# A decoder trunk on one core: the front starts from the normalised input, and the residual is transposed in the output projection

## The chip, the core and the metric

The kernel runs on one core of one Trainium2 chip. The metric is device time of one execution in microseconds (us). An engine in the text is one of the core's five instruction streams, each of which works its list in order: PE (TensorE: products and transposes), DVE (VectorE), ACT (ScalarE), POOL (GpSimd) and SP (SyncE, which only issues DMAs; ACT and POOL can issue some too).

## What is computed

Two layers over 1024 tokens of width 1024, with 16 learned "meta" tokens put ahead of them (1040 in all). This change touches the first half of layer 0, a Mamba-2 mixer with its RMS norm:

```python
h = concat([meta, x])                         # 1040 x 1024
u = rmsnorm(h, ssd_norm)                      # h * rsqrt(mean(h*h) + eps) * gain
z, xbc, dt_raw = split(u @ w_in, ...)         # 2048, 3072 and 32 columns
xbc = silu(causal_dwconv(xbc))
dt = softplus(dt_raw + dt_bias)               # the time steps, one per token and head
...                                           # state space scan, gate, group norm
h = h + hg @ w_out                            # 2048 -> 1024: the output projection
```

The rest (the gated FFNs, the attention of layer 1, the last norm) is the same in both kernels.

## The kernel before

**Layout.** Activations lie feature-major: 128 features on the partitions, tokens along the free axis. The tokens are cut into three *tiles* of 348, 348 and 344 (`TT`), and each tile into three *chunks* of 116 (`CH`, nine chunks c0 to c8). Every float32 product is made of three passes of a faster format: an operand is split into a high part and a low remainder (`uh`, `ul`; `wh`, `wl` for weights), and `mm3` (L193 to L195) multiplies high by high, high by low and low by high. ACT writes the high parts, DVE (for activations) or POOL (for weights, L98, in quarters) the remainders.

**The front (`load_x`).** The nine chunks of x arrive token-major, in two DMAs each (112 rows and 4, `by_rows`, L405), the odd ones from SP's queue and the even ones from ACT's own. For each tile, `stream(j)` squares the three chunks with a sum along the row (L364 on DVE, L366 on ACT), transposes the *raw* chunks on PE (L371, eight groups k of 128 features, three transposes each), copies them out of PSUM as `h` (L374 and L376) and multiplies `h` by the 32 columns `wdt` of the time steps as a plain float32 product (L377, into `dtr`). With the third tile, the finished rows `h` go to DRAM as `h0_d` (L379), eight rows of 520 KB. `token_rstd` turns the sums into one factor per token (L244 to L250). Then `scaled(j)` multiplies the chunks by their factors (L388), transposes them again (L393, into `xr`) and writes `uh` (L303, ACT) and `ul` (L304, DVE), the operands of the input projection. The time steps, made from raw rows, are multiplied by the factors later, in `dt_path` (L460).

**After the front.** `stream` (the method at L603) runs the input projection block by block: a block is 128 output columns, three tiles of 24 products (`pj`, L193 to L195), then a convolution (one ACT instruction L320, three DVE instructions L323) and a silu (L512). Group 0 has six blocks. Between them `dt_path` makes the decays: `acs` (L480), `end` (L481), a transposition `rows` (L493), a round over DRAM, and the tile `D`. The state space part begins with the first `cb` (L665) on PE, after 18 tiles of group 0 and one more tile of products; from there on a hand-written order mixes the scan with further projections.

**The output projection (`out_proj`).** Three passes g over eight row blocks f, each with three tiles of 12 products (`acc`). In the first pass `h[f]` is fetched from `h0_d` (L419), and every pass adds its products to `h[f]` on DVE (L431). A last stage on two halves of the tokens follows.

Outside the hand-written part, a scheduler places the instructions of each engine by its own estimate of when operands are there; what it made of the program is what the rows of order show. PSUM banks come from small pools: `mm` (2 banks), `sm` (3), `lg` (2), `ex` (1). The big SBUF rows are 28 slots of one pool (`Q`), the weights three slots of each kind.

Of the kernel before, what the change touches and what calls it, by code (L numbers as in the profile page):

```python
# [13 lines left out]
P = 128  # L14
D = 1024
# [54 lines left out]
ORD = ((0, 0), (1, 0), (0, 1), (1, 1), (0, 2), (1, 2))  # L70
# [3 lines left out]
PIECE = 256  # L74

# [25 lines left out]
class Trunk:  # L101
    def __init__(self, ctx, tc, a):
# [10 lines left out]
        self.open = []  # L113
        self.consts()
# [56 lines left out]
    def load_w(self, src, n, gain=None, out=None):  # L171
# [8 lines left out]
        nc.scalar.activation(wh[:, :n], w32[:, :n], AF.Copy)  # L180
# [9 lines left out]
    def mm3(self, out, wh, wl, uh, ul, first, last, joins=False, tie=None):  # L190

        mm = self.nc.tensor.matmul
        self.behind(mm(out, wh, uh, start=first, stop=False, skip_group_check=joins), tie, "behind the sums of squares")  # L193
        mm(out, wh, ul, start=False, stop=False, skip_group_check=joins)  # L194
        mm(out, wl, uh, start=False, stop=last, skip_group_check=joins)  # L195
# [41 lines left out]
    def token_rstd(self, ss, m, k, eps=EPS, y=None, src=None):  # L237
# [6 lines left out]
        nc.vector.tensor_scalar(ss[:m, :k], (ss if src is None else src)[:m, :k], 1.0 / D, eps, op0=ALU.mult, op1=ALU.add)  # L244
        nc.scalar.activation(y[:m, :k], ss[:m, :k], AF.Ln)
        nc.scalar.activation(y[:m, :k], y[:m, :k], AF.Exp, scale=-0.5)
# [48 lines left out]
    def parts(self, t, u, s0, n, g, eng=None):  # L295
# [6 lines left out]
        else:  # L302
            nc.scalar.activation(h, t, AF.Copy, scale=g)  # L303
            nc.vector.scalar_tensor_tensor(l, t, g, h.bitcast(F32), op0=ALU.mult, op1=ALU.subtract)  # L304
# [22 lines left out]
    def load_x(self, pool, mx):  # L327
# [5 lines left out]
        wdt = self.wp.tile([P, 1024], F32, tag="w32", name="wdt")  # L333
        self.ln_exp()
        d = self.dp.tile([KD, P, L], F32, tag="h0_d", name="h0_d")
        r9 = mx.tile([P, 3, 3], F32, tag="r9", name="r9")
        dt = self.ex("dtr")
        xs = []
        for c, (t0, n) in enumerate(CH):
# [4 lines left out]
            else:  # L344
                self.by_rows(nc.sync if c % 2 else nc.scalar, xt[:n, :], a["x"][t0 - META : t0 - META + n, :], n)
            if c == 0:
                nc.sync.dma_start(wdt[:, : KD * H], a["w_dt"])
                v = wdt[:, : KD * H].rearrange("p (k h) -> p k h", k=KD)
                nc.gpsimd.tensor_tensor(v, v, self.par("ssd_norm", 0, KD).unsqueeze(2).to_broadcast([P, KD, H]), op=ALU.mult)
# [4 lines left out]
        hs = [self.Q("h") for _ in range(KD)]  # L354

        def stream(j):
            s0, nn = TT[j]
            x3 = xs[3 * j : 3 * j + 3]
            for i in range(3):
                c = 3 * j + i  # L360
                n = CH[c][1]
                t = self.wp.tile([P, D], F32, tag="wl", name=self.nm("junk"))
                if c in SQD:
                    nc.vector.scalar_tensor_tensor(t[:n, :], x3[i][:n, :], 1.0, x3[i][:n, :], op0=ALU.mult, op1=ALU.mult, accum_out=ss[:n, c : c + 1])  # L364
                else:
                    nc.scalar.activation(t[:n, :], x3[i][:n, :], AF.Square, accum_out=ss[:n, c : c + 1])  # L366
            for k in range(KD):
                ps = self.lg("xT")
                for i in range(3):
                    n = CH[3 * j + i][1]  # L370
                    nc.tensor.transpose(ps[:, i * CB : i * CB + n], x3[i][:n, k * P : k * P + P], self.ident[:n, :n])  # L371
                h = hs[k][:, s0 : s0 + nn]
                if k % 2:
                    nc.scalar.activation(h, ps[:, :nn], AF.Copy)  # L374
                else:
                    nc.vector.tensor_copy(h, ps[:, :nn])  # L376
                nc.tensor.matmul(dt[j * H : j * H + H, :nn], wdt[:, k * H : k * H + H], h, start=k == 0, stop=k == KD - 1)  # L377
                if j == 2:
                    nc.sync.dma_start(d[k], hs[k][:, :L])  # L379
            self.token_rstd(ss[:, 3 * j : 3 * j + 3], CB, 3, y=r9[:, :, j])  # L380

        def scaled(j):
            s0, nn = TT[j]
            x3 = xs[3 * j : 3 * j + 3]
            for i, t in enumerate(x3):
                n = CH[3 * j + i][1]
                r = r9[:n, i : i + 1, j]
                nc.vector.tensor_scalar(t[:n, :], t[:n, :], r, None, op0=ALU.mult)  # L388
            for k in range(KD):
                ps = self.sm("xr")  # L390
                for i in range(3):
                    n = CH[3 * j + i][1]
                    nc.tensor.transpose(ps[:, i * CB : i * CB + n], x3[i][:n, k * P : k * P + P], self.ident[:n, :n])  # L393
                self.parts(ps[:, :nn], u[k], s0, nn, self.par("ssd_norm", k))

        for step, j in ORD:
            (scaled if step else stream)(j)
        return d, u, dt, r9
# [25 lines left out]
    def accumulate(self, h, f, s0, n, w, ks, front=0, bank=None, base=0):  # L424
# [6 lines left out]
        self.nc.vector.tensor_tensor(h[f][:, o], h[f][:, o], ps[:, :n], op=ALU.add)  # L431


    def dt_path(self, ps, r9, cp):
# [168 lines left out]
    def stream(self, blocks, w0=None):  # L603
# [11 lines left out]
        for n in range(3 * len(todo)):  # L615
# [5 lines left out]
            if n in calls:  # L621
                calls.pop(n)()
# [1208 lines left out]
```

## Time and profile before

| what | value |
|---|---|
| three runs, us | 2891.38, 2893.07, 2890.8 (median 2891.38) |
| the profiled execution, us | 2892.33 |
| its span (first to last instruction), us | 2890.5 |
| PE busy | 2834.6 us, 98% of the span |
| DVE busy | 2096.3 us, 73% |
| ACT and POOL busy | 1628.0 us and 1610.4 us, 56% each |
| mean granted PE clock | 0.997 |
| DMA | 278.70 MB, 90 GB/s of HBM traffic over the span |

The span is 1.8 us shorter than the execution's own time: what lies around the first and the last instruction. The profile lists busy time by engine, the span in 40 slices, the chain of work that ended last, the groups of instructions by source line, and who waited for whom. A row of the timeline gives the start, the duration, the engine, the line, the operation, output<-input, and how often it stands there in sequence; in brackets the idle time before it and what ended that. The end of a product is modelled and reaches into the next one, so that the step from start to start is what a product costs in a row.

### The profile page before, as it was taken

How to read it: one execution, taken by the hardware profiler on the slowest of the kernel's cores; microseconds unless marked ns; L12 is line 12 of the kernel's file. 1: busy time of each engine (PE TensorE's matmuls, PEld its weight loads, DVE VectorE, ACT ScalarE, POOL GpSimd, SP SyncE). 2: the span in 40 equal slices, each digit the busy share in tenths (PEclk: the TensorE clock that was granted, in tenths of full speed). 3: DMA queues.
4: the chain of work that ended last, by engine and by line, in shares of the span. 5: the costliest groups of instructions: out<-in, count | busy, mean ns of one | idle time of the engine just before them, and what ended most of it. 6: DMA issues, size and time to landing. Idle time of an engine off the chain costs nothing. (4 is left out here: it accounts for less than half of the span.)

```text
span 2890.5 us, 58592 instructions
## 1 busy us (share of the span) xinstructions
PE 2834.6 (98%) x21835; PEld 2701.9 (93%) x21835; DVE 2096.3 (73%) x4044; ACT 1628.0 (56%) x3392; POOL 1610.4 (56%) x2430
## 2 busy tenths in 40 slices
PE   7999999999999999999999999999999999999998
PEld 4999999999999999999999999999798999999888
DVE  5676666668387667666886888888749776767776
ACT  4455544544265656565335888888736565555433
POOL 2265555552429888858743222222363888885882
PEclk9999999999999999999999999999999999999999
DMA  5233333343213222244132222222332222225331
GB/s 168 75 107 95 117 94 117 114 156 135 81 60 97 81 81 76 81 161 164 52 114 78 57 68 66 62 63 54 134 117 74 81 76 79 81 81 183 110 102 66
DMA packets 128265, 278.70 MB, mean 96 GB/s; under 512 B 14787, under 2 KB 58828, under 8 KB 127980
## 3 DMA queue, kind: packets, MB, share of 16 engines
q1 hardware_dynamic: 122028, 261.70, 28.7%
q10 hardware_dynamic: 4112, 6.56, 0.7%
q0 software_dynamic: 1840, 6.70, 0.6%
q8 instruction: 172, 2.82, 0.4%
q14 instruction: 113, 0.93, 0.1%
HBM read 204.63 MB, written 55.36 MB: 90 GB/s over the span
## 5 line engine op out<-in xcount | busy, mean ns | idle before, releaser
L98 POOL TENSOR_TENSOR wl<-w,wh 128x256 fp32r<-128x256 f32 x768 | 682.0, 918 | 377.3 <-ACT wh L180 299.8
L193 PE MATMUL pj<-uh,wh 128*128 128x348 f32 (+2 forms) x1536 | 500.0, 326 | 2.7 <-DVE qs L1469 1.9
L194 PE MATMUL pj<-ul,wh 128*128 128x348 f32 (+2 forms) x1536 | 494.7, 322 | 0.0
L195 PE MATMUL pj<-uh,wl 128*128 128x348 f32 (+2 forms) x1536 | 491.5, 320 | 0.0
L193 PE MATMUL p<-bh,fh 128*128 128x262 f32 (+1 forms) x1408 | 400.4, 285 | 5.5 <-DVE p L1118 5.5
L195 PE MATMUL p<-bh,fl 128*128 128x262 f32 (+1 forms) x1408 | 400.1, 284 | 1.9 <-POOL fl L98 1.9
L194 PE MATMUL p<-bl,fh 128*128 128x262 f32 (+1 forms) x1408 | 398.7, 283 | 0.0
L98 POOL TENSOR_TENSOR fl<-x,fh 128x256 fp32r<-128x256 f32 x352 | 265.6, 786 | 191.9 <-ACT fh L1055 161.5
L193 PE MATMUL p<-bh,wh 128*128 128x262 f32 (+1 forms) x1040 | 295.7, 284 | 1.5 <-ACT ft L1115 1.5
L194 PE MATMUL p<-bl,wh 128*128 128x262 f32 (+1 forms) x1040 | 295.8, 284 | 1.2 <-DVE bl L979 1.2
L195 PE MATMUL p<-bh,wl 128*128 128x262 f32 (+1 forms) x1040 | 295.0, 284 | 0.0
L193 PEld LDWEIGHTS pj<-uh,wh 128*128 128x128 f32 x1536 | 288.3, 188 | 5.0 <-issue 1.9
L194 PEld LDWEIGHTS pj<-ul,wh 128*128 128x128 f32 x1536 | 288.9, 188 | 1.1
L195 PEld LDWEIGHTS pj<-uh,wl 128*128 128x128 f32 x1536 | 288.6, 188 | 0.6 <-issue 0.6
L323 DVE SCALAR_TENSOR_TENSOR c<-p,params,c 128x260 f32<-128x260 f32 (+1 forms) x528 | 248.5, 480 | 53.3 <-ACT c L320 46.7
L193 PEld LDWEIGHTS p<-bh,fh 128*128 128x128 f32 x1408 | 267.1, 190 | 6.3 <-DVE p L1118 5.9
L195 PEld LDWEIGHTS p<-bh,fl 128*128 128x128 f32 x1408 | 267.0, 190 | 2.8 <-POOL fl L98 2.5
L194 PEld LDWEIGHTS p<-bl,fh 128*128 128x128 f32 x1408 | 267.5, 190 | 0.1
L1115 ACT ACTIVATE ft<-p 128x262 f32<-128x262 f32 (+1 forms) x352 | 132.5, 382 | 175.0 <-DVE p L1118 111.2
L195 PE MATMUL acc<-gh,wl 128*128 128x260 f32 (+1 forms) x672 | 213.5, 320 | 2.8 <-POOL wl L98 2.6
L193 PE MATMUL acc<-gh,wh 128*128 128x260 f32 (+1 forms) x672 | 210.9, 320 | 3.1 <-DVE h L1279 3.1
L194 PE MATMUL acc<-gl,wh 128*128 128x260 f32 (+1 forms) x672 | 213.9, 319 | 0.0
(332 smaller groups left out, 7898.9 us busy)
## 6 DMA issues: line engine op xcount, KB each, us to landing
w<-in_w_up SPq DMA_DIRECT2D x88, 512.0 KB
w<-in_w_down SPq DMA_DIRECT2D x44, 512.0 KB
w<-in_w_in SPq DMA_DIRECT2D x40, 512.0 KB
E<-ea_d SPq DMA_DIRECT2D x32, 464.0 KB
D<-acs_d SPq DMA_DIRECT2D x32, 420.5 KB
g<-c SPq DMA_DIRECT2D x88, 130.0 KB
g<-c SPq DMA_DIRECT2D x88, 128.0 KB
b<-g SPq DMA_DIRECT2D x16, 520.0 KB
```

What stands on the lines that cost most here:

```text
L98: eng.tensor_tensor(out[:, c], x[:, c], y[:, c], op=op)
L193: self.behind(mm(out, wh, uh, start=first, stop=False, skip_group_check=joins), tie, "behind the sums of squares")
L194: mm(out, wh, ul, start=False, stop=False, skip_group_check=joins)
L195: mm(out, wl, uh, start=False, stop=last, skip_group_check=joins)
L323: ins = nc.vector.scalar_tensor_tensor(out, ps[:, o + i : o + i + n], wcol(i), out, op0=ALU.mult, op1=ALU.add)
L1115: nc.scalar.activation(s[:, :N], ps[:, :N], AF.Copy)
```

## The change

1. **The raw pass goes.** L371, L374, L376, L377 and the eight stores L379 are no longer there, nor the multiplication by the factors in `dt_path`. Instead the 32 columns of the time steps are split into high and low parts (`wd`, laid into zeroed tiles with 96 columns per product, so that each token tile lands in its own 32 rows of `dtr`), and multiplied by `uh` and `ul` with `mm3`: 24 products per tile, 72 in all.
2. **Order of loads.** The first three chunks, then the first weight block and `w_dt`, then the other six chunks. ACT issues only c0 and c2; SP issues everything else.
3. **Tile by tile.** A generator (`steps`) makes tile j: factors for two chunks, then for the third; chunks scaled in place, shared by DVE and ACT; eight transposition groups; `uh` and `ul`. The squares of the next tile are placed between them. Between tiles stand one tile of products of the first block, and the time-step products. Ordering ties (`behind`) hold the scheduler to this.
4. **The residual.** `h[f]` in the first pass is copied from PSUM (`new`). In the second and third pass the input x is read a second time, in feature blocks of 128 columns (`load_rows`, eight DMAs in pieces of 512 bytes), eight 128x128 transposes per block put it into two PSUM banks (`add_rows`), and DVE adds it to `h[f]`. The meta tokens go over a small DRAM tile, `meta_d`.

What it does to the order. PE's list begins as follows before (`x_108`, `x_114`, `x_117` are the chunks of tile 0; `xT` the raw transposes, `xr` the scaled ones), first its start, and then the place where the first block begins:

```order
L371 MATMUL xT_183<-ident,x_108 128x116
L371 MATMUL xT_189<-ident,x_108 128x116
L371 MATMUL xT_183<-ident,x_114 128x116
L371 MATMUL xT_189<-ident,x_114 128x116
L371 MATMUL xT_183<-ident,x_117 128x116
L371 MATMUL xT_189<-ident,x_117 128x116
L377 MATMUL dtr_107<-h_169,wdt 32x348
```

```order
L193 MATMUL pj_549<-uh_137,wh_532 128x352
L377 MATMUL dtr_107<-h_171,wdt 32x348
L371 MATMUL xT_320<-ident,x_120 128x116
L371 MATMUL xT_320<-ident,x_123 128x116
L371 MATMUL xT_320<-ident,x_126 128x116
L393 MATMUL xr_260<-ident,x_108 128x116
L393 MATMUL xr_260<-ident,x_114 128x116
L393 MATMUL xr_260<-ident,x_117 128x116
L194 MATMUL pj_549<-ul_138,wh_532 128x352
```

In the changed kernel (`x_106`, `x_110`, `x_113` are tile 0, `xr` its scaled transposes) PE's list has, after eight small transposes of the meta tokens:

```order
L402 MATMUL xr_221<-ident,x_113 128x116
L402 MATMUL xr_227<-ident,x_113 128x116
L402 MATMUL xr_233<-ident,x_113 128x116
L195 MATMUL pj_280<-uh_139,wh_118 128x352
L402 MATMUL xr_239<-ident,x_106 128x116
L402 MATMUL xr_239<-ident,x_110 128x116
L402 MATMUL xr_239<-ident,x_113 128x116
L196 MATMUL pj_280<-ul_140,wh_118 128x352
L197 MATMUL pj_280<-uh_139,wl_119 128x352
L195 MATMUL pj_280<-uh_141,wh_118 128x352
```

The raw transposes and the float32 products are gone from between the block's products; the first block's first tile follows the first tile's scaled transposes directly, and the 24 products into `dtr` stand behind it.

ACT's list before: five DMAs more than in the changed kernel stand ahead of its first square.

```order
L405 DMA x_117<-in_x 4x1024
L405 DMA x_123<-in_x 112x1024
L405 DMA x_123<-in_x 4x1024
L405 DMA x_129<-in_x 112x1024
L405 DMA x_129<-in_x 4x1024
L405 DMA x_135<-in_x 112x1024
L366 ACTIVATE junk_177,ss_101<-x_108 116x1024
```

And in the changed kernel, with the path of the third chunk (`x_113`) behind the copy of the first weights:

```order
L491 DMA x_113<-in_x 4x1024
L377 ACTIVATE junk_190,ss_101<-x_106 116x1024
L433 ACTIVATE mT_186<-mT_177 128x128
L247 ACTIVATE r_104<-ss_101 116x2
L248 ACTIVATE r_104<-r_104 116x2
L377 ACTIVATE junk_194,ss_101<-x_113 116x1024
L247 ACTIVATE r_104<-ss_101 116x1
L248 ACTIVATE r_104<-r_104 116x1
L417 ACTIVATE wh_118<-w_0_116 128x1024
L394 ACTIVATE x_113<-x_113,r_104 116x512
```

ACT's first square is no longer behind the issue of later chunks; those DMAs stand in SP's list.

SP's list of the changed kernel, in the third pass of the output projection: the six blocks of x that this pass adds (`xb`) stand together, ahead of the pass's last three weight loads.

```order
L466 DMA xb_7834<-in_x 128x8x128
L466 DMA xb_7837<-in_x 128x8x128
L466 DMA xb_7902<-in_x 128x8x128
L466 DMA xb_7905<-in_x 128x8x128
L176 DMA w_1006_8113<-in_w_out_f 128x512
L176 DMA w_1012_8162<-in_w_out_f 128x512
L176 DMA w_1018_8211<-in_w_out_f 128x512
```

The core of the diff:

```diff
+LOADS = {(1, 0): (0, 1), (2, 0): (2, 3), (2, 1): (4, 5), (2, 2): (6, 7)}
+ADDS = {(1, 2): (0,), (1, 3): (1,), (2, 1): (2,), (2, 2): (3, 4), (2, 3): (5, 6), (2, 4): (7,)}
...
+        for c in range(3):
+            load(c)
+        w32 = self.wp.tile([P, 1024], F32, tag="w32", name="w32_0")
+        nc.sync.dma_start(w32, first)
...
+        nc.sync.dma_start(wdt, a["w_dt"])
+        for c in range(3, 9):
+            load(c)
...
+        def tile(j):
+            a, b, c = range(3 * j, 3 * j + 3)
+            if j == 0:
+                for x in (a, b, c):
+                    square(x, None)
+            factors(j, 0, 2)
+            scale(a, [(nc.vector, 0, D)])
+            factors(j, 2, 1)
+            scale(b, [(nc.scalar if j else nc.vector, 0, D)], None if j else self.first_factor)
+            if j == 0:
+                self.behind(nc.scalar.activation(w0[0], w32, AF.Copy), self.last_exp, "behind the factors")
+                pieces(nc.gpsimd, w0[1], w32, w0[0].bitcast(F32), ALU.subtract)
+            scale(c, [(nc.vector, 0, D // 2), (nc.scalar, D // 2, D)])
+            transposed(j, range(KD // 2))
+            if j < 2:
+                hi, lo = made[j, KD // 2 - 1]
+                square(a + 3, hi)
+                square(b + 3, lo)
+            transposed(j, range(KD // 2, KD))
+            if j < 2:
+                square(c + 3, made[j, KD - 1][0])
...
+            for j in range(3):
+                s0, n = TT[j]
+                c = slice(HALO + s0, HALO + s0 + n)
+                for k in range(KD):
+                    w = slice(2 * H + G * k - H * j, 2 * H + G * k - H * j + G)
+                    self.mm3(dt[:G, :n], wd[0][:, w], wd[1][:, w], u[k][0][:, c], u[k][1][:, c], j == k == 0, j == 2 and k == KD - 1, tie=self.last_mm)
+                if j < 2:
+                    tile(j + 1)
...
+    def load_rows(self, f):
+        t = self.Q("xb")
+        self.nc.sync.dma_start(t[:, :SEQ].rearrange("p (c q) -> p c q", q=P), self.a["x"][:, f * P : f * P + P].rearrange("(c p) q -> p c q", p=P))
+        self.nc.gpsimd.dma_start(t[:, SEQ : SEQ + META], self.meta_d[f])
+        return t
+
+    def add_rows(self, h, t):
+        nc = self.nc
+        banks = [self.sm("xT") for _ in range(2)]
+        tie = self.last_mm
+        for c in range(SEQ // P):
+            ins = nc.tensor.transpose(banks[c // 4][:, c % 4 * P : c % 4 * P + P], t[:, c * P : c * P + P], self.ident)
+            self.behind(ins, tie, "behind the block's products")
+            tie = None
+        m = h[:, HB : HB + META]
+        nc.vector.tensor_tensor(m, m, t[:, SEQ : SEQ + META], op=ALU.add)
+        for i, ps in enumerate(banks):
+            x = h[:, HB + META + 512 * i : HB + META + 512 * i + 512]
+            nc.vector.tensor_tensor(x, x, ps, op=ALU.add)
...
-        self.nc.vector.tensor_tensor(h[f][:, o], h[f][:, o], ps[:, :n], op=ALU.add)
+        if new:
+            self.nc.vector.tensor_copy(h[f][:, o], ps[:, :n])
+        else:
+            self.nc.vector.tensor_tensor(h[f][:, o], h[f][:, o], ps[:, :n], op=ALU.add)
...
             u, dt, heads, w0, front = self.load_x(pool, mx, self.a["w_in"][DI // P])
             dt = self.dt_path(dt, heads, mx)
             next(front)
             rows = [[] for _ in range(4)]
             group = self.stream(self.in_group(u, 0, rows[0]), w0, True)
             for _ in range(3):
                 next(group)
                 next(front)
             next(dt)
...
                 if g == 0:
-                    h[f] = self.fetch(hd[f], "h", front=HB)
+                    h[f] = self.Q("h")
+                    self.nc.gpsimd.tensor_copy(h[f][:, :HB], self.zero[:, :HB])
+                for k in LOADS.get((g, f), ()):
+                    rows[k] = self.load_rows(k)
...
+                for k in ADDS.get((g, f), ()):
+                    self.add_rows(h[k], rows.pop(k))
```

More of the change, by code (lines that the diff above doesn't have):

```diff
@@ L382, in scaled @@
[L382 to L394, printed above, removed]
@@ L396, in load_x, with square @@
-        for step, j in ORD:
-            (scaled if step else stream)(j)
-        return d, u, dt, r9
+        G = 3 * H
+        wd = [self.Q("wd", F32R) for _ in range(2)]
+        for t in wd:
+            nc.gpsimd.memset(t.bitcast(F32), 0.0)
+        taps = [t[:, 2 * H : 2 * H + KD * G].rearrange("p (k h) -> p k h", h=G)[:, :, :H] for t in wd]
+        made = {}
+        def square(c, tie):
+            n = CH[c][1]
+            t = self.wp.tile([P, D], F32, tag="wl", name=self.nm("junk"))
+            x, acc = xs[c][:n, :], ss[:n, c : c + 1]
+            if c in SQD:
+                ins = nc.vector.scalar_tensor_tensor(t[:n, :], x, 1.0, x, op0=ALU.mult, op1=ALU.mult, accum_out=acc)
+            else:
+                ins = nc.scalar.activation(t[:n, :], x, AF.Square, accum_out=acc)
+            self.behind(ins, tie, "behind the tile in front")
@@ new lines, in transposed @@
+        def transposed(j, ks):
+            s0, nn = TT[j]
+            for k in ks:
+                ps = self.sm("xr")
+                for i, x in enumerate(xs[3 * j : 3 * j + 3]):
+                    n = CH[3 * j + i][1]
+                    t = nc.tensor.transpose(ps[:, i * CB : i * CB + n], x[:n, k * P : k * P + P], self.ident[:n, :n])
+                    if j:
+                        self.behind(t, self.last_mm, "behind the products in front")
+                made[j, k] = self.parts(ps[:, :nn], u[k], s0, nn, self.par("ssd_norm", k))
@@ L797, in mixer @@
                     pass
[L798 removed]
+        return rows[3][:4], yd, list(zip(y0[1], y0[0]))
     def fetch_y(self, d):
```

136 lines of the change are left out of this document (74 added, 62 removed).

## The prediction

> **What bounds the kernel now.** I read the page first, then who waited for whom on PE, then the timeline at the start.
>
> ```profile
> PE 2834.6 (98%) x21835; PEld 2701.9 (93%) x21835; DVE 2096.3 (73%) x4044; ACT 1628.0 (56%) x3392; POOL 1610.4 (56%) x2430
> ...
> PE   7999999999999999999999999999999999999998
> ```
>
> PE is busy nearly always; the first slice (72 us) alone shows less. So two things count here: when PE gets useful work at the start, and how much PE work there is. PE's longest waits, over the whole run:
>
> ```profile
> PE xT L371 <- DMA x<-in_x: 10.7, 2, 5.8
> ...
> PE dtr L377 <- ACT h L374: 3.0, 1, 3.0
> ...
> PE acc L193 <- DVE h L431: 0.6, 2, 0.4
> ```
>
> The first two stand in the front, the third in the first pass of the output projection. PE's timeline of the front, and where the scan begins:
>
> ```profile
> 14.09 0.84 PE L371 MATMUL xT<-ident,x 116*128 116x116 f32 x3
> 17.94 1.37 PE L377 MATMUL dtr<-h,wdt 128*32 128x348 f32 x2 [3.01 <-ACT h L374]
> ...
> 24.91 0.52 PE L371 MATMUL xT<-ident,x 116*128 116x116 f32 x3
> ...
> 28.72 0.46 PE L393 MATMUL xr<-ident,x 116*128 116x116 f32 x3
> ...
> 32.78 0.40 PE L193 MATMUL pj<-uh,wh 128*128 128x352 f32 x1
> ...
> 35.19 0.77 PE L377 MATMUL dtr<-h,wdt 128*32 128x348 f32 x2
> 35.90 0.52 PE L371 MATMUL xT<-ident,x 116*128 116x116 f32 x3
> ...
> 36.25 0.46 PE L393 MATMUL xr<-ident,x 116*128 116x116 f32 x3
> ...
> 131.01 0.33 PE L195 MATMUL pj<-uh,wl 128*128 128x352 f32 x1
> 131.18 0.27 PE L665 MATMUL cb<-ident,xbc 128*116 128x128 f32 x1
> ...
> 131.49 0.60 PE L669 MATMUL px<-ident,xbc 128*116 128x128 f32 x4
> 131.84 0.41 PE L193 MATMUL pj<-uh,wh 128*128 128x352 f32 x1
> ```
>
> The scaled transposes begin at 28.7 and the first `cb` stands at 131.2; PE is dense between, 102.5 us. Two prices are read here: a product costs 0.16 from start to start, and four 128x128 transposes 0.35, with the product behind them 0.41 long, about 0.1 more. Three transposes took 0.84 at 14.1 and 0.52 at 24.9: PE runs slow until about 24.2, though the granted clock of that stretch is recorded as 1.00 (the column ahead of the DMA share in the next fence).
>
> **The end of the front, before and after.** `cb` comes after 18 tiles of group 0 and one more in both programs, and the code from there on is the same. So the front's gain is how much earlier PE reaches it.
>
> *Removed from the dense stretch:* the raw groups.
>
> ```profile
> 0.00:28.70 28.70, 6.89 (x30) 1.00 0.75 200
> 28.70:62.00 33.30, 7.36 (x44) 1.00 0.46 177
> ```
>
> ```profile
> 28.70:62.00 33.30, 11.75 (x32) 1.00 0.46 177
> ```
>
> These are L371 (two stretches) and L377. The busy times, 7.4 + 11.8 = 19.1 us, overlap with neighbours and are the upper bound. From start to start a raw group costs 0.71 (35.19 to 35.90) and 0.35 (to 36.25), 1.06 in all, of which 0.1 is the switch to other work, which partly stays; 16 of the 24 `dtr` products (two recorded instructions each) stand in this stretch: 17.0 us, and 15.4 without the switch, the lower bound. I take 17.0, since steps are what PE spends. 85.5 remain.
>
> *Added:* 72 products for the time steps at 0.16 = 11.5 us, all on PE in this stretch, with no cover.
>
> *The new start.* Landing is read from the queue, where a load waits for a slot of an earlier one:
>
> ```profile
> 0.84 14.41 ACTq L405 DMA_DIRECT2D x<-in_x  x9
> ...
> 10.68 0.31 SPq L405 DMA_DIRECT2D x<-in_x  x1
> 11.01 0.32 ACTq L405 DMA_DIRECT2D x<-in_x  x1
> ...
> 15.36 1.06 ACT L366 ACTIVATE junk<-x 116x1024 f32<-116x1024 f32 x1 [13.27 <-DMA x<-in_x]
> ```
>
> The second and third chunks landed just before 10.68 and 11.01. ACT's first square ran at 15.4 only because its own DMA issues stood ahead of it; in the new order four issues do. The weight block now travels beside these chunks in place of two later ones, much the same bytes, so I take 10.4 and 10.9. Then the chain runs on these prices:
>
> ```profile
> 12.64 1.22 DVE L364 SCALAR_TENSOR_TENSOR junk<-x 116x1024 f32<-116x1024 f32 x1
> ...
> 19.05 0.21 ACT L246 ACTIVATE r<-r 116x3 f32<-116x3 f32 x1
> ...
> 19.68 0.17 DVE L249 TENSOR_SCALAR tb<-tb 116x3 f32<-116x3 f32 x1
> 19.88 0.16 DVE L250 TENSOR_TENSOR r<-r,tb 116x3 f32<-116x3 f32 x1
> ...
> 26.97 1.05 ACT L180 ACTIVATE wh<-w 128x1024 fp32r<-128x1024 f32 x1
> ```
>
> ```profile
> L388 DVE TENSOR_SCALAR x<-x,r x9: 742/752/1292, 26.6 to 58.1; 116x1024 f32<-116x1024 f32 x8, 112x1024 f32<-112x1024 f32 x1
> ```
>
> Square of c1 with its read-out 1.3 (11.7), sum, logarithm and exponential 0.2 each (12.3), four small DVE steps at 0.2 (13.1), two chunks scaled at 0.75 with the next sum between (14.8). Meanwhile ACT squares c2 (to 13.6), makes its factor (14.4) and copies the weights (15.4); four DVE steps (15.6), two half scales (16.2), transposes, first `uh`: **first product at 17.2**, against 32.8 before.
>
> From 17.2, at slow PE prices (0.84 a group of transposes, 0.32 a product), tile 0 still needs five groups and 24 products, 4.2 + 7.7 = 11.9. Before, PE sped up 6.2 us after its dense run began (17.94 to about 24.2). The same here: 6.2 slow, then 5.7 at half price, 2.9: tile 0's projection ends at 26.2. The suppliers are no slower than that once PE is fast:
>
> ```profile
> L304 DVE SCALAR_TENSOR_TENSOR ul<-xr,params,uh 128x348 fp32r<-128x348 f32 (+1 forms) x24 | 13.3, 570 | 8.8 <-ACT uh L303 8.8
> ```
>
> That is 0.57 a group, about 0.49 from start to start in a row. [...]
>
> *Sum.* Done by 26.2 are 24 products (3.8) and eight groups of scaled transposes. A group costs at least 0.25 + 0.08 for the switch, and at most
>
> ```profile
> 28.70:73.00 44.30, 11.46 (x72) 8.44 (x72) 1.00 0.38 145
> ```
>
> 11.46 / 24 = 0.48; I take 0.37, 3.0 us. So 85.5 + 11.5 - 6.8 = 90.2 remain, plus 0.7, since ACT makes the second block's weights between two of tile 1's `uh`: `cb` at 26.2 + 90.9 = 117.1, **14.1 us earlier**. Cover between tiles: tile 0's time-step products (24 x 0.16 = 3.8 us) hide the scaling of tile 1's last chunk, which by the same prices ends within 0.3 of them; nothing is left over, and what DVE or ACT lose there, PE loses. Tile 2 has the second block's products as cover. I allow 0 to 4 us here. The decays' round over DRAM has cover too:
>
> ```profile
> 103.59 0.70 SPq L637 DMA_DIRECT2D D<-acs_d  x2
> ...
> 133.78 1.60 DVE L648 TENSOR_SCALAR D<-D,cols 116x116 f32<-116x116 f32 x8
> ```
>
> `D` was asked for 27.6 us before `cb`; in the new order PE's `rows` stands 123 rows ahead of `cb` rather than 195, which at 0.16 a row leaves 27.6 - 11.5, about 16.
>
> **The output projection.** Added on PE: 64 transposes, eight blocks of 0.70 + 0.1 = 0.8 us, 6.5 in all. Bounds: 5.6 (steps alone) and 9.6 (0.60 per four). PE is full there, so nothing hides them. DVE's two adds per block (0.5 to 0.7 each) are covered:
>
> ```profile
> 700.00:720.00 20.00, 20.00 (x129) 20.00 (x128) 18.16 (x35) 7.61 (x15) 6.77 (x9) 1.00 0.19 56
> 720.00:740.00 20.00, 20.00 (x129) 20.00 (x128) 6.11 (x12) 3.51 (x7) 4.29 (x6) 1.00 0.18 53
> ```
>
> DVE (third busy column) has 1.8 us free in the first stretch, 14 in the second, and five PSUM banks hold 9 us of products. The first pass loses its 4.2 MB of reloads, and I count 0.3 of the 0.6 us wait as gone.
>
> **Net:** -14.1 + 6.5 - 0.3 = -7.9 us from the profiled 2892.33, 2884.4. That execution is 0.95 above the median 2891.38, so I predict **2883.5** for the median.
>
> [...]
>
> **Rivals.**
> - *PE stays slow through tile 0.* Half of PE's time there goes to transposes. The end is then 29.1 rather than 26.2: 2886.4. Against it: it sped up before in a stretch that was 40% transposes (0.84 of 2.07).
> - *DVE sets the pace of tiles 1 and 2.* Per tile it has 8 x 0.49 + 1.3 + 0.75 + 0.4 + 8 x 0.2 + 2 x 0.2 + 3 x 0.49 = 9.8 us, against PE's 48 x 0.16 + 3.0 = 10.7. At the worst prices above (1.29 per scale, 0.57 per `ul`, and 0.33 for half of the small steps) it is 12, and two tiles cost some 3 to 4 us: 2887.
> [...]
> - *Slower: the second reading of x stalls the third pass.* Its six blocks stand in SP's list ahead of the last three weights and can't start before the second pass has freed their slots. The last is needed after five blocks, 180 products or 28.8 us later. At the mean price of a piece,
>
> ```profile
> q1 hardware_dynamic: 122028, 261.70, 28.7%
> ```
>
> 0.287 x 16 x 2890.5 / 122028 = 0.109 us, 1024 pieces over 16 engines take 7.0 us and six blocks 42: a stall of 13, 2896.5. It begins at 0.075 us a piece and eats the gain at 0.095. Against it, the round of the decays in pieces of 464 bytes (100.7 to 103.6):
>
> ```profile
> q1 hardware_dynamic: 473, 0.19, 28.3%
> ```
>
> 0.283 x 16 x 2.9 / 473 = 0.028 us, so 1.8 us a block.
>
> **Chances.** Forecast (2880 to 2887) 0.50; better 0.17; DVE's pace 0.13; slow tile 0 0.12; stalled third pass 0.08. A measurement of this kernel can tell 0.2%, 5.8 us, from no change, so the border is 2885.6: 0.10 of the forecast's chance lies above it. Faster 0.40 + 0.17 = 0.57, within 0.10 + 0.13 + 0.12 = 0.35, slower 0.08. The range takes in the better case and the two small losses with the 4 us allowance: 2878 to 2891; it leaves out the stall and tails.
>
> **What would show it.** First `pj` at about 17, tile 0's last at about 26, 24 `dtr` products (96 rows) behind it, `cb` at about 117, no PE wait over 1 us between 26 and 117; each block of residual transposes 0.7 to 0.9, with no DMA wait ahead of it. I am wrong if PE waits for `uh`, `ul` or scaled chunks between the tiles, if transposes in the output projection wait for `xb`, or if `cb` comes early and the gain is given back behind it.

## The result and the profile after

The changed kernel took **2883.53 us** (median of 8 runs, 2880.12 to 2884.9), the kernel before 2890.53 (8 runs on the same chip): a ratio of 0.9973, 95% interval 0.9962 to 0.9984, 7.0 us less. The forecast was 2883.5. The profiled execution took 2880.28 us (span 2878.6), which is 12.05 us less than the profiled execution of before. So the pair of profiles shows more than the medians, and the first question is where the other 5 us stand.

The page of the changed kernel:

```profile
PE 2826.2 (98%) x21859; PEld 2710.5 (94%) x21859; DVE 2093.7 (73%) x4068; ACT 1630.2 (57%) x3393; POOL 1626.2 (56%) x2440
...
PE   8999999999999999999999999999999999999998
```

The first slice rose from 7 to 8 tenths; nothing else can be seen at this grain. The windows view, PE alone, cut where the same work starts in both programs (first `cb`; first `acc<-y`, the output projection; first sum of squares behind it; and on). The columns are the stretch, its length, PE's busy time with its instructions, the granted clock (the share of its full clock that PE had, as the profile records it), the DMA share and GB/s. Before:

```profile
0.00:131.20 131.20, 114.95 (x659) 1.00 0.44 132
131.20:645.60 514.40, 511.62 (x3844) 1.00 0.37 109
645.60:801.50 155.90, 155.29 (x1009) 1.00 0.37 120
801.50:1298.20 496.70, 493.50 (x3996) 1.00 0.27 89
1298.20:1555.60 257.40, 250.93 (x2030) 1.00 0.33 111
...
2079.40:2190.50 111.10, 110.28 (x868) 0.99 0.36 121
```

After:

```profile
0.00:116.30 116.30, 100.75 (x618) 1.00 0.40 108
116.30:631.10 514.80, 511.89 (x3845) 1.00 0.37 109
631.10:794.30 163.20, 162.55 (x1073) 1.00 0.39 119
794.30:1290.30 496.00, 492.03 (x3996) 1.00 0.27 89
1290.30:1545.30 255.00, 250.22 (x2030) 1.00 0.34 112
...
2068.70:2178.40 109.70, 108.75 (x868) 1.00 0.36 123
```

Read down the lengths. The front is 14.9 us shorter, the scan the same, the output projection 7.3 longer. That is a gain of 7.2 at 794 us, and there the changed code ends. Nearly all the rest of the 12 us is 0.7, 2.4 and 1.4 us in three stretches that the change doesn't touch, one of them with a granted clock of 0.99 before and 1.00 after (the two stretches left out differ by 0.4 and 0.2). Whether that is chance is the control's question below.

The timeline of the changed front, ACT's and DVE's squares first, then PE:

```profile
7.69 1.23 DVE L375 SCALAR_TENSOR_TENSOR junk<-x 116x1024 f32<-116x1024 f32 x1 [6.54 <-DMA x<-in_x]
...
12.43 1.06 ACT L377 ACTIVATE junk<-x 116x1024 f32<-116x1024 f32 x1 [2.76 <-DMA x<-in_x]
...
15.65 0.84 PE L402 MATMUL xr<-ident,x 116*128 116x116 f32 x3 [0.32 <-DVE x L392]
...
16.75 0.66 PE L195 MATMUL pj<-uh,wh 128*128 128x352 f32 x1 [0.25 <-ACT uh L305]
...
22.76 0.43 PE L197 MATMUL pj<-uh,wl 128*128 128x352 f32 x1
23.03 0.32 PE L195 MATMUL pj<-uh,wh 128*128 128x352 f32 x1
...
25.68 0.32 PE L195 MATMUL dtr<-uh,wd 128*96 128x348 f32 x1
...
80.34 0.40 PE L195 MATMUL pj<-uh,wh 128*128 128x348 f32 x1 [1.40 <-DVE xbc L325]
...
116.35 0.27 PE L751 MATMUL cb<-ident,xbc 128*116 128x128 f32 x1
```

The second chunk landed at about 7.6, the third at 12.4: its square on ACT waited for the DMA, and everything up to the first product at 16.75 hangs on it. PE runs at half rate (0.29 from one product's start to the next, later 0.16) until about 23.0, and tile 0's products end at 25.68. PE's waits up to 130 us:

```profile
PE xr L402 <- DVE x L392: 8.3, 3, 5.7
PE mT L431 <- POOL ident L154: 4.6, 1, 4.6
PE pj L195 <- DVE xbc L325: 1.4, 1, 1.4
```

The first two lie ahead of the first product. Behind it PE waits for little but the convolution (`xbc`, L325) at 80 us.

### The profile page after: what moved, and what is told of

Same layout as the page of the kernel before. It is cut to its first block, busy times and chain, and to the rows that moved or that the text cites. A ratio compares the mean times of both kernels' runs of the same rounds, so it can differ in the third digit from the quotient of the medians.

```text
span 2878.6 us, 58687 instructions
## 1 busy us (share of the span) xinstructions
PE 2826.2 (98%) x21859; PEld 2710.5 (94%) x21859; DVE 2093.7 (73%) x4068; ACT 1630.2 (57%) x3393; POOL 1626.2 (56%) x2440
## 4 chain that ended last, share of the span: by engine, by line
PE 45%; DVE 2%; ACT 1%; POOL 1%; issue 1%; DMA 0%; ACTq 0%; DVEq 0%; SPq 0%; POOLq 0%
PE p L197 5%; PE p L195 5%; PE p L196 5%; PE acc L197 4%; PE acc L195 4%; PE acc L196 4%; PE pj L195 3%; PE pj L196 3%; PE pj L197 3%; PE po L1658 3%; PE lg L1617 3%; PE wT L1644 3%; POOL wl L99 1%; DVE h L1071 0%; ACT bt L1621 0%
## 5 line engine op out<-in xcount | busy, mean ns | idle before, releaser
L325 DVE SCALAR_TENSOR_TENSOR c<-p,params,c 128x260 f32<-128x260 f32 (+1 forms) x528 | 248.5, 480 | 54.9 <-ACT c L322 48.4
```

The costliest lines, as they stand in the source:

```text
L325: ins = nc.vector.scalar_tensor_tensor(out, ps[:, o + i : o + i + n], wcol(i), out, op0=ALU.mult, op1=ALU.add)
```

## The experiments

The theory from the trace: the front gains because PE has its first product 16 us earlier, and because of the raw work that left against the time-step products that came; the residual costs its transposes on PE; nothing else counts. The rivals: the residual's price is DMA; the time-step products are cover rather than cost; the clock or DVE sets the front's pace; the stages behind take part.

### The changed kernel once more

No edit.

> The changed kernel once more, unchanged, as the control of this set and for the spread of its runs. Its profiled run was 12 us faster than that of the kernel before; 7.2 us of them stand before 840 us, the other 4.9 in stages whose instructions are the same. Theory 1 (those 4.9 us are chance: stretches of lower granted clock behind waits at the joints of stages): cb at 116.4 again, passes 163 again, median 2882 to 2885, and whatever differs by the end goes with the mean granted clock, about 2 us for 0.001. Theory 2 (the change makes later stages faster): the same 10 us or more gained at the later marks in this profile too.

Measured: 2881.29 us (2879.88 to 2884.25, 5 runs), ratio 0.9966 (0.9953 to 0.9978). Its profile:

```profile
631.30:794.50 163.20, 162.54 (x1072) 1.00 0.39 119
...
1290.50:1547.00 256.50, 250.43 (x2030) 1.00 0.33 111
...
2070.80:2182.20 111.40, 110.62 (x868) 0.97 0.35 121
```

`cb` stands at 116.6, and the ends of the changed parts repeat to 0.3 us; 1.5 and 1.7 of the others' gain is gone, one with a clock of 0.97. So these two are chance, theory 1: **the changed code is worth 7.2 us in the profiled pair.** The medians say 7.0 in the first set and 10.1 in this one, each against the kernel before on the same chip, so a gain of some us behind the changed code isn't excluded. Over the 13 runs of the two sets the time goes with the run's mean granted clock: 2880.4 at 0.998 (mean of 4), 2882.3 at 0.997 (3), 2884.3 at 0.996 and 0.995 (6). The kernel before took 2891.0 at 0.997 (mean of the 48 runs with that clock beside the experiments), 8.7 above the changed kernel's 2882.3.

### The residual left out, the residual alone, its loads alone

```
-LOADS = {(1, 0): (0, 1), (2, 0): (2, 3), (2, 1): (4, 5), (2, 2): (6, 7)}
-ADDS = {(1, 2): (0,), (1, 3): (1,), (2, 1): (2,), (2, 2): (3, 4), (2, 3): (5, 6), (2, 4): (7,)}
+LOADS = {}
+ADDS = {}
```

> The changed kernel with the residual left out: the input is neither read a second time nor added, so the output lacks that term. It prices the output projection's part. Theory 1 (the residual costs the steps of its 64 transposes on a full PE, 8 x 0.8): the passes are 6 to 8 us shorter than the 163.8 us of the changed kernel, cb stays at 116.4, total near 2876.5. Theory 2 (the 7.7 us by which the passes grew are partly DMA pieces or adds that hold up PE): also shorter by 7.7, but then PE's rows around the transposes in the changed kernel must show gaps larger than the transposes themselves. Theory 3 (the time is given back elsewhere, other stages fill it): the passes shorten, the total does not.

Measured: 2875.45 us, ratio 0.9953 (0.994 to 0.9965), cb at 115.9, the passes 156.1 us (630.7 to 786.8), 7.1 shorter. PE around a block's transposes in the changed kernel (start, duration):

```profile
696.84 1.03 PE L477 MATMUL xT<-ident,xb 128*128 128x128 f32 x8
697.63 0.41 PE L195 MATMUL acc<-yh,wh 128*128 128x348 f32 x1
697.88 0.32 PE L196 MATMUL acc<-y,wh 128*128 128x348 f32 x1
```

Eight transposes take 0.79 from start to start, and the product behind them 0.25 in place of 0.16: 0.88 a block, 7.0 for eight. That is the whole difference, with no wait in it: theory 1. (PE waits 0.7 for `h` in these passes with and without the residual.)

Next, the kernel before with the new residual and its own front (the lines that fall away: the stores of `h0_d` and its fetch in the first pass):

```
-                if j == 2:
-                    nc.sync.dma_start(d[k], hs[k][:, :L])
+                if j == 0:
+                    nc.sync.dma_start(self.meta_d[k], hs[k][:, :META])
...
-                    h[f] = self.fetch(hd[f], "h", front=HB)
+                    h[f] = self.Q("h")
...
+                for k in ADDS.get((g, f), ()):
+                    self.add_rows(h[k], held.pop(k))
```

> The kernel before with the second half of the change alone: its own front (raw transposes kept, nothing stored for later but the 16 meta tokens), the residual transposed and added in the second and third pass. If the two parts simply add: cb at 131.2 as before, the passes 7.7 us longer, total 2890.5 + 6 to 8 = 2896.5 to 2898.5. Rival: the eight stores of 524 KB in the front or the eight reloads in the first pass cost PE something too; then cb comes up to 1 us earlier or the first pass is shorter, and the total is under 2895.

Measured: 2897.13 us, ratio 1.0023 (1.0013 to 1.0033), 5.8 slower than before. Its passes take 163.3 (643.8 to 807.1), 7.4 longer; its cb stands at 129.4, 1.8 earlier. The chunks had landed some 0.5 earlier, and PE was at full rate from about 21.2 rather than 24.2; so the 1.8 is no saving of the stores, as far as these rows show, but the spread of a slow start (below). The two halves add: 14.9 of the front less 7.1 to 7.4 of the residual, against 7.2 for both.

Last, the loads with nearly nothing done to them:

```
-                    self.add_rows(h[k], rows.pop(k))
+                    t, m = rows.pop(k), h[k][:, HB : HB + META]
+                    self.nc.vector.tensor_tensor(m, m, t[:, SEQ : SEQ + META], op=ALU.add)
+                    m = h[k][:, HB + META : HB + 2 * META]
+                    self.nc.vector.tensor_tensor(m, m, t[:, :META], op=ALU.add)
```

> The changed kernel with the second reading of the input kept, in the same 512-byte pieces, but without the 64 transposes and their adds (only two strips of 16 columns of each block are added, so that the residual is left out but for those). Theory 1 (the transposes' steps on PE are the whole price): the passes take 156 us as in the run without the residual. Theory 2 (the pieces on the DMA engines hold up weights or rows): some of the 7.1 us stays, 157 to 163.

Measured: 2874.84 us, ratio 0.9942 (0.9928 to 0.9955), the passes 157.5 us (630.5 to 788.0). Of the 1.4 above the run without residual, 0.7 is two waits of PE for an add (`acc` for `h`, L520) that the other lacks; at most the other 0.7 can be the DMA's. So the pieces of 512 bytes are at most a tenth of the 7.1.

### The time-step products: one in place of three

```
-                    self.mm3(dt[:G, :n], wd[0][:, w], wd[1][:, w], u[k][0][:, c], u[k][1][:, c], ...)
+                    one = nc.tensor.matmul(dt[:G, :n], wd[0][:, w], u[k][0][:, c], ...)
+                    self.behind(one, self.last_mm, "behind the products in front")
+                    self.last_mm = one
```

> The changed kernel with one product per time-step row block in place of three (the two low-order products are left out, so the time steps are less exact): 48 products of 0.157 us fewer, 7.5 us. Theory 1 (all of them stand on PE's path with no cover): cb comes 7.5 us earlier, at 108.8, and PE does not wait between the tiles. Theory 2 (they are the cover under which the next tile's chunks are scaled): tile 0's 16 products (2.5 us) come back as a wait for scaled chunks and so do part of the following 16; cb at 111 to 113. Theory 3 (DVE sets the pace once PE has less): waits on uh and ul through tiles 1 and 2, cb at 112 to 114.

Measured: 2887.57 us, ratio 0.9989 (0.998 to 0.9998), 4 to 6 us **slower** than the changed kernel's two medians with 48 products fewer; cb at 116.5. The windows of the two around tile 1, PE alone, the changed kernel first:

```profile
29.00:32.00 3.00, 2.37 (x18) 1.00 0.02 8
32.00:35.00 3.00, 3.00 (x23) 1.00 0.01 3
```

And with one product in place of three:

```profile
29.00:32.00 3.00, 1.74 (x10) 1.00 0.01 3
32.00:35.00 3.00, 3.00 (x15) 0.52 0.03 8
```

Without cover PE waited 1.68 for a scaled chunk at 29.6, was busy for 1.74 of 3 us, and then ran at half rate for about 3 us. So this wait cost itself and a slow stretch behind it. At 78.9 PE waited 4.0 for the convolution, and a second slow stretch (a clock of 0.83 in 80 to 90) followed. This gives back all 7.5 us, more than theory 2 had, and the mean clock fell to 0.994. (The shorter front also moved the written order of the last feed-forward, of which more below.)

The cover kept, tile 0 with its 24 products, tiles 1 and 2 with 8:

```
+                    if j == 0:
+                        self.mm3(dt[:G, :n], wd[0][:, w], wd[1][:, w], u[k][0][:, c], u[k][1][:, c], k == 0, False, tie=self.last_mm)
+                        continue
```

> As the run with one product in place of three (time steps less exact), but only for tiles 1 and 2; tile 0 keeps its 24. 32 products of 0.157 us fewer, 5.0 us. Theory 1 (tile 0's products are the cover for scaling tile 1's chunks, and the waits and the slow stretch behind them were the whole loss of that run): cb 4 to 5 us earlier than in the changed kernel, 111.4 to 112.4. Theory 2 (DVE's pace limits the front besides: the wait for the convolution at 80 us grew from 1.4 to 4.0): that wait grows again, cb at 114 or later.

Measured: 2883.54 us, ratio 0.9976 (0.9967 to 0.9985), cb at 115.8. No wait for chunks over 0.3 us and no slow stretch in tile 1 (a clock of 1.00 from 25.6 to 42 us); PE reached the end of the time-step products 4.8 us earlier (61.5 against 66.3). It lost that at the convolution, in PE's timeline:

```profile
78.24 0.40 PE L195 MATMUL pj<-uh,wh 128*128 128x348 f32 x1 [4.00 <-DVE xbc L325]
...
79.81 0.49 PE L197 MATMUL pj<-uh,wl 128*128 128x348 f32 x1
80.10 0.49 PE L195 MATMUL pj<-uh,wh 128*128 128x348 f32 x1
...
82.71 0.34 PE L195 MATMUL pj<-uh,wh 128*128 128x348 f32 x1
```

The step between starts is 0.29 for 3 us behind the wait, where it was 0.16. DVE, which PE waits for, in the same kernel:

```profile
69.43 0.31 DVE L553 TENSOR_SCALAR dt<-dt 116x288 f32<-116x288 f32 x1 [2.27 <-ACT dt L552]
69.77 1.95 DVE L554 RECIPROCAL dt<-dt 116x288 f32<-116x288 f32 x1
...
74.31 0.56 DVE L325 SCALAR_TENSOR_TENSOR xbc<-pj,params,xbc 128x344 f32<-128x344 f32 x1
```

The chain that makes the time steps stands in front of the convolution's three DVE instructions (L325), and DVE is busy for 9.86 of the 10 us from 70 to 80 (6.53 in the changed kernel). Theory 2: on tiles 1 and 2 the products are not cover for chunks, but the DVE chain behind them binds next, with 1.4 us of wait already in the changed kernel.

### The third chunk earlier

```
-                self.by_rows(nc.scalar if c == 2 else nc.sync, xt[:n, :], ...)
+                self.by_rows(nc.sync, xt[:n, :], ...)
...
-                for x in (a, b, c):
-                    square(x, None)
+                square(a, None)
+                square(b, None)
             factors(j, 0, 2)
+            if j == 0:
+                square(c, self.last_exp)
```

> The changed kernel with the third chunk's load on the same queue as the second's, right behind it and ahead of the first weight block, and its square behind the first two factors. Theory 1 (the third chunk's late landing, 12.4 us, sets when PE starts): it lands at 9 to 10.5, first product at 14 to 15.2 in place of 16.75. Theory 2 (bytes in all queues set the landing, whatever the order): it lands at 12 or later, no change or a loss. For the slow first stretch: if PE speeds up a fixed time after its dense run begins (6.3 us), cb comes as much earlier as the first product, 1.5 to 2.7 us; if it speeds up at a fixed time of the program (23 to 24 us in both kernels so far), only half of that is kept, 0.8 to 1.4 us.

Measured: 2882.86 us (2879.49 to 2887.47), ratio 0.997 (0.9961 to 0.998). The third chunk's square starts at 10.49, then PE's timeline:

```profile
14.81 0.66 PE L195 MATMUL pj<-uh,wh 128*128 128x352 f32 x1 [0.25 <-ACT uh L305]
...
19.93 0.78 PE L402 MATMUL xr<-ident,x 116*128 116x116 f32 x3
21.39 0.46 PE L402 MATMUL xr<-ident,x 116*128 116x116 f32 x3
23.55 0.32 PE L195 MATMUL dtr<-uh,wd 128*96 128x348 f32 x1
```

First product 1.9 earlier, full rate at about 21.2 and so not at a fixed time of the program, cb at 114.3, 2.0 earlier. Theory 1 for the landing. Full rate came 6.4 after the first product, much as in the changed kernel, but the other profiles show that this delay isn't fixed (3.7 to 6.4, listed with tile 0's end below). The total can't be told from the changed kernel's.

### PE kept busy ahead of tile 0

Products of a constant by itself fill PE's wait; the counts differ between the five kernels, three of which have the early third chunk as well:

```
+        pw = self.sm("warm")
+        def warm(n, tie):
+            for _ in range(n):
+                ins = nc.tensor.matmul(pw[:, :P], self.ones, self.ones, start=True, stop=True)
+                self.behind(ins, tie, "fills the wait")
+                tie = ins
+            return tie
+        warm(72, None)
...
+                    elif k == 0:
+                        if i:
+                            self.behind(t, self.filled, "behind the filling")
+                        self.filled = warm((30, 8, 0)[i], t)
```

> The changed kernel with 110 products of a constant by itself on PE while it waits for the first tile (72 ahead of the first scaled transposes, 30 and 8 in the next two gaps); their result is not used. Theory 1 (PE runs slow for the first 6.3 us of dense work, whatever the work): PE is fast when the first product comes at 16.75, tile 0's last product at 22.3 to 23 in place of 25.5, cb 2.5 to 3.1 us earlier, about 113.5. Theory 2 (DVE and ACT set tile 0's pace): waits for uh and ul appear and less than 1 us is gained. Theory 3 (the short gaps let it fall back to half rate): no gain.

Measured: 2892.1 us, ratio 1.0004 (0.9995 to 1.0012), cb at 127.1. I had mis-sized the filling, as PE's timeline shows:

```profile
8.62 12.10 PE L440 MATMUL warm<-ones 128*128 128x128 f32 x106
...
30.17 0.42 PE L195 MATMUL pj<-uh,wh 128*128 128x352 f32 x1
...
36.40 0.32 PE L195 MATMUL dtr<-uh,wd 128*96 128x348 f32 x1
```

Each is recorded twice at 0.114, 0.23 a product; I had taken a transpose's step. Yet it tells what was asked: at full rate tile 0 takes 6.2 from first product to first `dtr`, against 8.9, so the slow start costs 2.7 us.

With the early third chunk, and 6 and 7 products in the gaps in place of 30 and 8:

> Both at once: the third chunk's load right behind the second's, and 85 products of a constant on PE ahead of tile 0. If the two gains add: first product at 14.6 to 14.9, cb at 116.4 - 2.0 - 2.9 = 111.5, total 4.9 us under the changed kernel at the same granted clock, 2878 to 2879. If DVE's pace or the supply of weights and chunks binds once tile 0 begins earlier (the waits of 1.4 us for the convolution and those for scaled chunks grow): cb at 113 to 114.5.

Measured: 2888.27 us, ratio 0.9987 (0.9978 to 0.9995), cb at 120.6 for the same reason; 6.2 us from first product to `dtr` again.

Without the early chunk, sized anew:

```
-        warm(72, None)
+        warm(27, None)
...
-                        self.filled = warm((30, 8, 0)[i], t)
+                        self.filled = warm((11, 2, 0)[i], t)
```

> The filling ahead of tile 0 again, sized by what it measured: one product of the constant took 0.23 us at full rate and 0.46 at half rate, where 0.09 and 0.18 were assumed, so the 110 of them kept PE until 29.3. Here 40: 27 ahead of the first scaled transposes, 11 and 2 in the gaps; they end by 11 and 14.5 by those prices. Theory 1 (PE is fast once it has been kept busy long enough; in the overfilled run the stretch from first product to the end of tile 0 was 6.2 us against 8.9): first product at 16.7, cb 2.5 to 2.7 us earlier, 113.7. Theory 3 (the idle gaps before the third chunk, about 0.5 us each, drop it to half rate again): no gain.

Measured: first product 16.27, first `dtr` 22.50, cb at **113.2**, 3.1 earlier: theory 1. But 2883.62 us, ratio 0.9974 (0.9964 to 0.9984).

With the early chunk, and 27, 2 and 2 products:

> The third chunk's load right behind the second's, with 31 products of the constant (27, 2, 2) ahead of tile 0. If both gains hold: first product at 14.6 to 14.9, cb at 116.4 - 2.0 - 2.7 = 111.7, and at the same granted clock a total of 4.7 us under the changed kernel, median about 2877 to 2879. If the wait for the convolution at 80 us takes some of it (the time steps' chain on DVE has less time before it): that wait grows from 1.4 us and cb comes at 112.5 to 114.

Measured: first product 15.40, cb at **112.6**, 3.7 earlier, the wait at the convolution still 1.4; 2881.66 us, ratio 0.9967 (0.9956 to 0.9979).

So up to 3.7 us gained at cb hardly show in the total. The starts of the same work in the profiled executions (us):

| | cb | 1st sum of squares | gate sums `acc<-gh` | `rt` | last `wT` | last sum of squares | last `p` | last `fin` |
|---|---|---|---|---|---|---|---|---|
| changed | 116.3 | 794.3 | 1290.3 | 1545.3 | 2068.7 | 2178.4 | 2632.0 | 2870.0 |
| changed, again | 116.6 | 794.5 | 1290.5 | 1547.0 | 2070.8 | 2182.2 | 2636.0 | 2874.0 |
| third chunk early | 114.3 | 792.2 | 1288.6 | 1545.2 | 2068.6 | 2179.5 | 2631.3 | 2869.2 |
| filled | 113.2 | 791.1 | 1288.5 | 1544.3 | 2067.8 | 2179.3 | 2635.1 | 2873.3 |
| filled, early | 112.6 | 790.5 | 1286.5 | 1543.2 | 2066.9 | 2178.4 | 2633.9 | 2871.8 |
| 36 products | 113.5 | 791.4 | 1288.8 | 1545.4 | 2069.2 | 2180.7 | 2634.3 | 2874.1 |

The two fillings take 455.8 and 455.5 from the last sum of squares to the last `p`, the changed kernel 453.6 and 453.8 (and the run with one product in place of three, whose order moved too, 456.1). Their waits there include one that the changed kernel lacks, the last of these (PE's waits, the filled kernel with the early chunk):

```profile
PE p L195 <- DVE p L1233: 3.6, 1, 3.6
PE p L197 <- POOL fl L99: 1.8, 1, 1.8
PE p L195 <- ACT fh L1170: 1.2, 1, 1.2
```

In both, the written order of that stage differs from the changed kernel's, though no line of it was edited: the order is planned from the front on. A last kernel, with 34, 1 and 1 products and the early chunk, asked whether that order is the loss:

> The third chunk early and 36 products of the constant (34, 1, 1) in place of 31 (27, 2, 2): so many that the written order of the last feed-forward, far behind, is again that of the changed kernel on every engine; in the two sized fillings it was another. There the gain at cb (3.1 and 3.7 us) was gone by the end: the stretch from the last sum of squares (near 2180) to the last p took 455.5 to 455.8 us, with a wait of 1.2 us for ACT's fh and a granted clock of 0.66 to 0.68 behind it, against 451.5 to 454.3 in the ten kernels without that order. Theory 1 (that order is the loss): no such wait, the stretch takes 451.5 to 454.3, cb near 112.6, median 2877 to 2880, some 3 us under the changed kernel. [...]

Measured: 2882.71 us (2877.65 to 2884.41), ratio 0.9959 (0.9945 to 0.9973). The stretch takes 453.6 and the wait for `fh` is gone: theory 1 for that stretch, some 2 us. But cb came at 113.5, the median is no better, and in the profiled execution (the slowest of the five) the time is lost elsewhere, some of it in the front (windows, PE alone):

```profile
14.00:16.00 2.00, 1.23 (x7) 1.00 1.02 234
16.00:18.00 2.00, 2.00 (x10) 0.55 1.04 242
...
20.00:22.00 2.00, 2.00 (x17) 1.00 1.01 256
```

PE, fast when it ended the filling, was thinly busy before 16 us and fell to half rate for 3.4 us (steps of 0.29 from 16.14 to 19.5). Two of its runs took 2877.7 and 2877.9 us at a clock of 0.997, three 2882.7 to 2884.4 at 0.995 and 0.996. No version was shown to beat the changed kernel: the medians of it and of the versions with an earlier `cb` all lie in 2881.3 to 2883.6. Where exactly their 2 to 4 us went in each run stays open; shown is that the one wait goes with the order, and that later stretches change by as much between two runs of one kernel. The order can't be all of it: in the filled kernel with the early chunk the last sum of squares, ahead of that stretch, already starts no earlier than in the first execution of the changed kernel (2178.4 both), though 3.8 earlier than in the control. A part goes with the clock: the two sized fillings ran at a mean of 0.9956 and 0.9955, the changed kernel's 13 runs at 0.9968, and by those runs 0.0012 is about 2 us, an estimate. What lowered it was not asked.

## Why the prediction was right, step by step

- **The new start, forecast 17.2, was 16.75, from two errors that offset, which is luck.** I put the second chunk at 10.4 and the third at 10.9; they landed at 7.6 and 12.4. By my sum ACT would have squared the third at 12.3, being held by the second's factors until then; it was free at 9.7 and waited for the chunk until 12.43. From that square to the first product I had 4.9 and it took 4.3. That the chunks would land as before with the weight block among them was the assumption that failed: behind the second chunk on its queue the third was squared at 10.49, and this brought 2.0 us at `cb`. Nor does the start repeat: in the control it was 17.74, a whole microsecond later, and `cb` only 0.3 later, because of the next point.
- **Tile 0's end, forecast 26.2, was 25.68.** PE slow for 6.2 us was taken from one execution, and 6.3 was met; but that is luck. From the first product to full rate it took 6.3, 4.0 (the control), 5.4 (no residual), 4.1 (cover kept), 6.4 (early chunk) and 3.7 (loads only). In the four fronts where PE sped up sooner (all but the early chunk's), it waited 0.4 to 0.5 for DVE ahead of the product that needs the last `ul`, so the tile ended at 25.0 to 25.9 anyhow: behind the slow start, DVE is the next limit of tile 0, within half a microsecond. What sets the delay, these runs don't show. The better case that the range takes in counted 1.6 us for PE at full rate sooner; that was my estimate and no run shows it: the runs showed these six delays and, where full rate came sooner, the wait for DVE. The rival of a slow tile 0, for which I had only the share of transposes in PE's work there, did not come: PE sped up within the tile in each of these six profiles. Transposes alone were not tested: they were busy for 3.2 of the slow 6.3 us, among products. With products alone, in the fillings, PE was slow for 3.4 to 5.4 us, much the same, by an estimate (their first 38 records took 6.04 to 7.05 us, 38 at 0.114 take 4.33, and at half rate the slow time is twice the excess).
- **From there to cb, forecast 90.9, was 90.7.** The raw groups' 17.0 and the products' 11.5 hold as a sum (from first product to cb it is 99.6 now and was 98.4); no run prices the raw groups by themselves. Taking products away showed that these 11.5 are not 11.5 to be won: tile 0's are cover (with 8 of the 24 PE waited 1.68 for a scaled chunk), and the DVE chain binds right behind the others (4.0 at the convolution).
- **The cover between the tiles** held: no wait over 0.5 there. The allowance of 0 to 4 us was met by the 1.4 at the convolution, which I did not name: I had counted DVE per tile, not the chain of the time steps on it at 70 to 80 us. My own mark "no PE wait over 1 us" failed by it.
- **The residual, forecast 6.5, was 7.1**, in the bounds: I took 0.70 + 0.1 a block, it is 0.79 + 0.09. The rival of the stalled third pass is out: no transpose waited for a load (PE's only listed wait in the passes is the 0.7 for `h`).
- **The first pass** kept its wait (0.7 against 0.6); my 0.3 for it was wrong.
- **The net** at the end of the changed code, forecast -7.9, was -7.2 in the profiled pair; the medians say -7.0, and -10.1 in the control's set.

## What to carry to other kernels

Judge a change of a few microseconds by the starts of the same work at the end of what was changed, in two profiles, before the total: here the marks at the end of the front and of the output projection repeated to 0.3 us, the totals spread over 5. Before taking work off a full engine, ask which other engine works under its cover; and where a schedule is planned from the front on, look whether an edit there has moved the order far behind.

## What the runs showed that was not expected

- A short wait can cost more than itself, but doesn't always. Behind waits of 1.7 and 4.0 us, and behind a thin stretch (1.23 busy of 2 us) without any gap over 0.6 us, PE ran at half rate for about 3 us (a product's step of 0.29 in place of 0.16). The recorded clock of the windows was 0.52 in 32 to 35 us behind the first, 0.83 and 0.86 in 80 to 90 behind the second (the runs with one product and with the cover kept), and 0.55 and 0.59 in 16 to 20 behind the thin stretch. Yet the changed kernel's wait of 1.4 us for the convolution left PE no busier and cost nothing but itself (windows, PE alone):

```profile
78.20:81.20 3.00, 1.60 (x10) 1.00 0.46 154
81.20:84.20 3.00, 3.00 (x21) 1.00 0.05 20
```

The sized filling, too, stayed at full rate behind a wait of 1.6 us, with PE busy for 1.41 of the 3 us ahead. So how busy PE was does not tell by itself whether a slow stretch follows; what does, these runs don't show.
- The half rate at the start is not in the recorded clock, which reads 1.00 from 0 to 23 us though a product's step is 0.29 there and 0.16 later; the later slow stretches are recorded (0.52 to 0.59 in windows of 2 and 3 us on them).
- One 128x128 product of plain f32 took 0.23 us at full rate, a transpose of that shape 0.10.
